# An input projection in 2x2x2 blocks with seven block products, and finished mixes kept in memory

## The chip, the core and the metric

The kernel runs on one core of a Trainium2 chip. The metric is the device time of one execution in microseconds. PE is TensorE (products), DVE is VectorE, ACT is ScalarE, POOL is GpSimd, SP is the engine that issues nearly all DMAs.

## What is computed

One layer of a decoder trunk on 1024 prompt tokens and 8 x 4 sample tokens, d = 1024:

```python
h = rmsnorm(x) * norm_g
b, c, u, z_a, v, z_b = split(h @ w_in)            # w_in: 1024 x 3072, six parts of 512
y_a = b * conv3(c * u) * silu(z_a)                # three taps, with the stored state for the samples
pooled = trailing_mean(v, windows 2/4/8/16) - v   # four groups of 128 channels
y_b = (pooled @ pool_w per group) * pool_scale * silu(z_b)
y = x + concat(y_a, y_b) @ w_out
out = rmsnorm(y) * final_g                        # and the new states of conv and pooling
```

All is float32. A product of two float32 operands is made of three products of the array: each operand is split into a high part of 12 bits and the rest (`split`: ACT copies the high part, DVE subtracts it), and high x low, low x high and high x high are summed.

## The kernel before

Channels lie on the partitions; the 1056 tokens are three thirds of 352 columns (`cols`). `w_in` has 24 column tiles of 128; for each tile and each third `project` issues 24 products (8 contraction chunks x 3 passes) into one PSUM bank, 72 per tile, 1728 in all. The order of the tiles is `M_ORDER`.

- Start: weights of the first three tiles and x arrive in slices by contraction chunk; ACT and DVE apply the gain to x and split it, third by third; PE works on the first three tiles slice by slice (`project_first`). ACT squares x, POOL adds the squares, a product with ones sums them over the channels (`sums_row`), and `rows_rsqrt` makes R, the inverse root mean square of every token, third by third. PE, ACT, DVE and POOL follow the written order in this stretch (`manual_schedule`); behind it a scheduler orders the instructions.
- Loop: tile i + 2 is loaded (512 KB, three buffers `wraw`) and split (three buffers `wt`) while tile i is multiplied. The evacuations multiply each bank by R (`evac`). Behind v come the windows, `pl` and the split `pooled`; behind u the taps `yc`; behind b the finished mix. `pool_linear` multiplies pooled by pool_w. A finished mix is split and stays in the buffers that x and the first weights left.
- Output: w_out is loaded and split per contraction chunk; five token tiles of 128 are done with tokens on the partitions (`po`, the first three together, chunk by chunk), the remaining 416 tokens with channels on the partitions (`pc`); then the residual, the final norm and the stores.

The lines below are those of the profile.

Of the kernel before, what the change touches and what calls it, by code (L numbers as in the profile page):

```python
# [19 lines left out]
NT = 3  # L20
# [33 lines left out]
def trunk(ctx, tc, xt, xres, xct, w_first, w_in, w_out, pool_w, par, fg, sconv, spool,  # L54
# [11 lines left out]
    def tmp(name):  # L66
        return tp.tile([P, TOK], F32, tag="tmp", name=name)
# [4 lines left out]
    # products of ones wake the array while the first operands arrive  # L72
# [6 lines left out]
    # six chunks (of contraction) by 352 tokens in each tile of x  # L79
    xraw = [big.tile([P, 6, TN], F32, tag="mix", name=f"xraw_{i}") for i in range(4)]  # L80

    def x_of(n, k, m=1):
        q = n * KD + k
        return xraw[q // 6][:, q % 6:q % 6 + m, :]

    def load_x(n, k, m):
        nc.sync.dma_start(x_of(n, k, m), xt[:, n * KD + k:n * KD + k + m, :])  # L87

    wfraw = {}

    def load_wf(k, m):
        if k % 2 == 0:
            pool, tag = (wp, "wraw") if k < 6 else (tp, "tmp")
            t = pool.tile([P, 2, WF], F32, tag=tag, name=f"wfraw_{k}")
            wfraw[k], wfraw[k + 1] = t[:, 0, :], t[:, 1, :]
            wfraw[k, 2] = t
        dst = wfraw[k, 2] if m == 2 else wfraw[k].rearrange("p (o c) -> p o c", o=1)
        nc.sync.dma_start(dst, w_first[:, k:k + m, :])  # L98

    for k, m in ((0, 1), (1, 1), (2, 1), (3, 1), (4, 2), (6, 2)):  # L100
        load_wf(k, m)
        load_x(0, k, m)
    load_x(1, 0, 4)
    load_x(1, 4, 4)
# [3 lines left out]
    def load_w(i):  # L108
        t = wp.tile([P, KD, P], F32, tag="wraw", name=f"wraw_{i}")
        nc.sync.dma_start(t, w_in[:, i - NF])  # L110
        wraw[i] = t

    load_x(2, 0, 2)
    load_x(2, 2, 6)
    load_w(NF)
# [8 lines left out]
    nc.vector.tensor_copy(onesr, ones)  # L124

    part = cst.tile([P, C_ALL], F32, name="part")
    nc.sync.dma_start(part, par)
    pwraw = wp.tile([P, NG, P], F32, tag="wraw", name="pwraw")
    nc.sync.dma_start(pwraw, pool_w)
    scb = cst.tile([P, NJ, 6 * NB], F32, name="scb")  # L130
    nc.sync.dma_start(scb[:, :, 0:2 * NB], sconv)
    spb = cst.tile([P, NG, 19 * NB], F32, name="spb")
    nc.sync.dma_start(spb[:, :, 0:15 * NB], spool)
    fgt = cst.tile([P, D], F32, name="fgt")
    nc.sync.dma_start(fgt, fg.partition_broadcast(P))
# [8 lines left out]

# [1 line left out]
    def split(dst, src):  # L146
        """dst[:, 0] = the top 12 bits of src, dst[:, 1] = the rest"""
        nc.scalar.activation(dst[:, 0], src, AF.Copy)  # L148
        nc.vector.tensor_tensor(dst[:, 1], src, dst[:, 0].bitcast(F32), op=ALU.subtract)  # L149

# [1 line left out]
    wfirst = [big.tile([P, 2, 2, NF * P], F32R, tag="mix", name=f"wf_{i}") for i in range(KD // 2)]  # L152
    wt = {}

    def w_of(i, a, k):
        if i < NF:
            return wfirst[k // 2][:, a, k % 2, i * P:(i + 1) * P]
        return wt[i][:, a, k, :]

    def split_w(i):  # L160
        t = wp.tile([P, 2, KD, P], F32R, tag="wt", name=f"wt_{i}")
        split(t, wraw.pop(i))
        wt[i] = t

# [1 line left out]
    xs = [big.tile([P, 2, TOK], F32R, tag="x", name=f"x_{k}") for k in range(KD)]  # L166
    gain = cst.tile([P, KD], F32, name="gain")

    def prep_x(n, k):
        c = cols[n]  # L170
        src = x_of(n, k)[:, 0, :]
        gk = wfraw[k][:, NF * P:] if n == 0 else gain[:, k:k + 1]
        nc.scalar.activation(xs[k][:, 0, c], src, AF.Copy, scale=gk)  # L173
        nc.vector.scalar_tensor_tensor(  # L174
            xs[k][:, 1, c], src, gk, xs[k][:, 0, c].bitcast(F32), op0=ALU.mult, op1=ALU.subtract)

    def prep_first(k):
        w = wfirst[k // 2][:, :, k % 2, :]
        split(w, wfraw[k][:, :NF * P])
        prep_x(0, k)  # L180
        nc.vector.tensor_copy(gain[:, k:k + 1], wfraw[k][:, NF * P:])

    acc = tmp("acc")

    def norm_x(n):
        for k in range(0, KD, 2):
            norm_pair(n, k)

    def norm_pair(n, k):
        c = cols[n]  # L190
        sq = tp.tile([P, 2, TN], F32, tag="tmp", name=f"sq_{n}_{k}")
        nc.scalar.activation(sq, x_of(n, k, 2), AF.Square)  # L192
        if k == 0:
            nc.gpsimd.tensor_tensor(acc[:, c], sq[:, 0], sq[:, 1], op=ALU.add)
        else:
            nc.gpsimd.tensor_tensor(sq[:, 0], sq[:, 0], sq[:, 1], op=ALU.add)
            nc.gpsimd.tensor_tensor(acc[:, c], acc[:, c], sq[:, 0], op=ALU.add)

    def sums_row(sums, name, whole=False):
# [3 lines left out]
        if whole:  # L203
            nc.tensor.matmul(pt, ones, sums, start=True, stop=True)
        else:
            two = tp.tile([P, 2, TC], F32R, tag="tmp", name=f"two_{name}")[:, :, :w]
            split(two, sums)
            for a in (1, 0):
                nc.tensor.matmul(pt, onesr, two[:, a], start=a == 1, stop=a == 0)  # L209
        return pt  # L210

    def rows_rsqrt(out, pt, name):
        """out = (pt / D + eps) ** -0.5, one Newton step behind the table's root;
        the generator lets other work in between the steps"""
# [3 lines left out]
        yield  # L218
        nc.vector.scalar_tensor_tensor(t, pt, D * EPS, out, op0=ALU.add, op1=ALU.mult)  # L219
        yield  # L220
        nc.vector.tensor_tensor(t, t, out, op=ALU.mult)
        yield
        nc.vector.tensor_scalar(t, t, -0.5 / D, 1.5, op0=ALU.mult, op1=ALU.add)
        yield
        nc.vector.tensor_tensor(out, out, t, op=ALU.mult)

# [1 line left out]
    pm = {}  # L228

    def product(i, n, k, a, b, start, stop):  # L230
        nc.tensor.matmul(pm[i, n], w_of(i, a, k), xs[k][:, b, cols[n]], start=start, stop=stop)  # L231

    def project(i, n):
        pm[i, n] = bank(f"pm_{i}_{n}")[:, :TN]
        seq = [(k, a, b) for k in range(KD) for a, b in ((0, 1), (1, 0))]
        seq += [(k, 0, 0) for k in range(KD)]
        for s, (k, a, b) in enumerate(seq):
            product(i, n, k, a, b, s == 0, s == len(seq) - 1)

    def project_first(n, k):  # L240
        if k == 0:
            for i in range(NF):
                pm[i, n] = bank(f"pm_{i}_{n}")[:, :TN]
        for s, (a, b) in enumerate(((0, 0), (1, 0), (0, 1))):
            for i in range(NF):
                product(i, n, k, a, b, k == 0 and s == 0, k == KD - 1 and s == 2)

    def evac1(i, n, out, in1):
        nc.vector.tensor_tensor(out[:, cols[n]], pm[i, n], in1[:, cols[n]], op=ALU.mult)  # L249

    def evac(i, out, in1):
        for n in range(NT):
            evac1(i, n, out, in1)

    mix = []

    def finish_mix(m, name):
        t = big.tile([P, 2, TOK], F32R, tag="mix", name=name)
        split(t, m)
        mix.append(t)  # L260

    def silu(z):
        nc.scalar.activation(z, z, AF.Silu)
        return z

    # group B
    pooled = {}
    szb = {}

    def after_v(g):  # L270
        w = 2 << g
        nc.scalar.copy(spb[:, g, 15 * NB:], vb[:, PM + SEQ:])
# [88 lines left out]
    def scale_rows(n, fill=()):  # L361
        """the rows of chunk n, with the calls of fill in between, then the evacuations"""
        fill = iter(fill)
        for _ in rows_rsqrt(R[:, cols[n]], pr[n], f"{n}"):
            f = next(fill, None)
            if f:
                f()
# [268 lines left out]
```

## Time and profile before

| | before |
|---|---|
| device time, median of 3 runs | 397.25 us (396.31 to 471.15) |
| span of the profiled execution | 394.9 us; its own time isn't listed, the two lower timed runs are 396.31 and 397.25 |
| PE busy | 384.5 us, 97% |
| DVE, ACT, POOL busy | 206.8, 103.8, 24.4 us |
| DMA moved | 31.49 MB |
| granted TensorE clock, mean | 0.990 |

A group of instructions in the profile gives its line, engine, operation, tiles and shape, the count, the busy time and the mean duration of one, and then the idle time just before them with what ended it. PE's products are pipelined: the busy time divided by the count is the pace, the mean duration is longer. The waits say who waited for whom, and the chain goes back from the last instruction through what released each.

### The profile page before, as it was taken

To read this page: it belongs to the slowest core of one execution; us is meant where nothing else is said; L and a number is where in the kernel's file an instruction comes from. 1 tells how busy PE (TensorE), PEld (TensorE's weight loads), DVE (VectorE), ACT (ScalarE), POOL (GpSimd) and SP (SyncE) were. 2 spreads that over 40 slices of the span, in tenths; PEclk is the share of its full clock that TensorE was granted. 3 is DMA by queue.
4 is the path that set the end of the run, shared out by engine and by line. 5 is a ranking of instruction groups with operands and counts; after the bars stand their busy time and mean duration, and the time that the engine had idled before them with its cause. 6 is when DMAs were issued, how large, how long until landed. Compare 5 with 4: busy or idle time off the path is not lost.

```text
span 394.9 us, 5304 instructions
## 1 busy us (share of the span) xinstructions
PE 384.5 (97%) x2238; PEld 370.6 (94%) x2238; DVE 206.8 (52%) x326; ACT 103.8 (26%) x166; POOL 24.4 (6%) x26
## 2 busy tenths in 40 slices
PE   8996999999999999999999999999999999999993
PEld 6996999999999999999999999999998889999883
DVE  4899669994925562326432163322536209322494
ACT  5982407241212230112221022212115106111211
POOL 0394500000000000000000000000000000000000
PEclk9998999999999999999999999999999999999997
DMA  7940131302111101111101111110178301200033
GB/s 245 414 157 1 56 106 55 106 4 78 55 53 56 53 2 53 55 53 55 53 7 48 53 55 53 55 43 15 54 263 296 95 0 54 108 0 0 2 149 130
DMA packets 11783, 31.49 MB, mean 80 GB/s; under 512 B 3568, under 2 KB 4720, under 8 KB 11632
## 3 DMA queue, kind: packets, MB, share of 16 engines
q1 hardware_dynamic: 11616, 30.83, 22.7%
q8 instruction: 17, 0.28, 0.3%
q10 hardware_dynamic: 144, 0.33, 0.2%
q14 instruction: 6, 0.05, 0.0%
HBM read 26.52 MB, written 4.64 MB: 79 GB/s over the span
## 4 chain that ended last, share of the span: by engine, by line
PE 89%; DVE 4%; ACT 2%; DMA 2%; issue 1%; SPq 1%; DVEq 0%
PE pm L231 64%; PE po L466 14%; PE pc L537 9%; DVE x L174 3%; DMA xraw<-in_xt_dram 2%; PE pp L304 1%; ACT x L173 1%; DVE R L217 1%; SPq L98 1%; SPq L87 0%; ACT wf L148 0%; PE pr L209 0%; ACT sq L192 0%; ACT po L475 0%; DVE rt L219 0%
## 5 line engine op out<-in xcount | busy, mean ns | idle before, releaser
L231 PE MATMUL pm<-x,wt 128*128 128x352 f32 x1512 | 244.3, 323 | 0.0
L231 PEld LDWEIGHTS pm<-x,wt 128*128 128x128 f32 x1512 | 243.5, 188 | 0.0
L148 ACT ACTIVATE wt<-wraw 128x1024 fp32r<-128x1024 f32 x21 | 22.2, 1059 | 139.4 <-PE pm L231 120.0
L231 PE MATMUL pm<-x,wf 128*128 128x352 f32 x216 | 38.6, 337 | 3.5 <-DVE x L174 3.1
L231 PEld LDWEIGHTS pm<-x,wf 128*128 128x128 f32 x216 | 36.4, 197 | 5.5 <-DVE x L174 3.9
L149 DVE TENSOR_TENSOR wt<-wraw,wt 128x1024 fp32r<-128x1024 f32 x21 | 25.7, 1223 | 10.1 <-ACT wt L148 10.1
L466 PE MATMUL po<-wo,mixa 128*128 128x512 f32 (+1 forms) x132 | 28.8, 374 | 0.0
L466 PE MATMUL po<-wo,mixb 128*128 128x512 f32 (+1 forms) x132 | 28.8, 373 | 0.0
L466 PEld LDWEIGHTS po<-wo,mixa 128*128 128x128 f32 x132 | 23.4, 189 | 4.5
L466 PEld LDWEIGHTS po<-wo,mixb 128*128 128x128 f32 x132 | 23.4, 189 | 4.4
L249 DVE TENSOR_TENSOR vb<-pm,t 128x352 f32<-128x352 f32 x12 | 6.3, 524 | 32.2 <-PE pm L231 32.2
L488 POOL TENSOR_TENSOR zg<-zt,fgt 128x256 f32<-128x256 f32 x1 | 0.7, 722 | 344.6 <-DVE zt L474 344.6
L249 DVE TENSOR_TENSOR t<-pm,R 128x352 f32<-128x352 f32 x12 | 6.3, 525 | 29.3 <-PE pm L231 29.3
L537 PE MATMUL pc<-mixb,wo 128*128 128x416 f32 x96 | 19.4, 351 | 0.0
L537 PE MATMUL pc<-mixa,wo 128*128 128x416 f32 x96 | 19.4, 350 | 0.0
L249 DVE TENSOR_TENSOR ya<-pm,sza 128x352 f32<-128x352 f32 x12 | 6.3, 524 | 25.0 <-PE pm L231 25.0
L474 DVE TENSOR_TENSOR zt<-po,zt 128x512 f32<-128x512 f32 (+1 forms) x11 | 7.0, 641 | 21.7 <-PE po L466 21.6
L537 PEld LDWEIGHTS pc<-mixb,wo 128*128 128x128 f32 x96 | 17.9, 188 | 0.3
L537 PEld LDWEIGHTS pc<-mixa,wo 128*128 128x128 f32 x96 | 18.0, 188 | 0.2
L174 DVE SCALAR_TENSOR_TENSOR x<-xraw,gain,x 128x352 fp32r<-128x352 f32 x16 | 17.3, 1136 | 0.4 <-ACT x L173 0.4
L148 ACT ACTIVATE wo<-woraw 128x1024 fp32r<-128x1024 f32 x8 | 8.3, 1057 | 32.7 <-PE pm L231 28.0
L475 ACT ACTIVATE po<-zt 128x512 f32<-128x512 f32 (+1 forms) x11 | 6.1, 557 | 33.6 <-DVE zt L474 33.6
(102 smaller groups left out, 271.4 us busy)
## 6 DMA issues: line engine op xcount, KB each, us to landing
wraw<-in_w_in_dram SPq DMA_DIRECT2D x21, 512.0 KB, 3.3
woraw<-in_w_out_dram SPq DMA_DIRECT2D x8, 512.0 KB, 3.6
zt<-in_xres_dram SPq DMA_DIRECT2D x5, 512.0 KB, 7.2
out_yt_dram<-zt SPq DMA_DIRECT2D x4, 512.0 KB, 2.6
xraw<-in_xt_dram SPq DMA_DIRECT2D x2, 704.0 KB, 8.1
xraw<-in_xt_dram SPq DMA_DIRECT2D x3, 352.0 KB, 6.7
xraw<-in_xt_dram SPq DMA_DIRECT2D x1, 1056.0 KB, 10.7
zc<-in_xct_dram SPq DMA_DIRECT2D x1, 832.0 KB, 4.4
```

What stands on the lines that cost most here:

```text
L98: nc.sync.dma_start(dst, w_first[:, k:k + m, :])
L148: nc.scalar.activation(dst[:, 0], src, AF.Copy)
L149: nc.vector.tensor_tensor(dst[:, 1], src, dst[:, 0].bitcast(F32), op=ALU.subtract)
L173: nc.scalar.activation(xs[k][:, 0, c], src, AF.Copy, scale=gk)
L174: nc.vector.scalar_tensor_tensor(xs[k][:, 1, c], src, gk, xs[k][:, 0, c].bitcast(F32), op0=ALU.mult, op1=ALU.subtract)
L217: nc.vector.reciprocal(out, t)
L231: nc.tensor.matmul(pm[i, n], w_of(i, a, k), xs[k][:, b, cols[n]], start=start, stop=stop)
L249: nc.vector.tensor_tensor(out[:, cols[n]], pm[i, n], in1[:, cols[n]], op=ALU.mult)
L466: nc.tensor.matmul(pt, mix[k][:, b, t * P:(t + 1) * P], wo[k][:, a, c], start=(k == 0 and s == 0), stop=(k == KD - 1 and s == 2))
L474: nc.vector.tensor_tensor(z[:, c], pt, z[:, c], op=ALU.add)
L475: nc.scalar.activation(pt, z[:, c], AF.Square, accum_out=ss[:, i:i + 1])
L537: nc.tensor.matmul(pt, wo[k][:, a, d * P:(d + 1) * P], mix[k][:, b, T0:], start=(k == 0 and s == 0), stop=(k == KD - 1 and s == 2))
```

## The change

The first two column tiles (v 0 and zb 0, `NF = 2`) are done as before, but with the gain applied to the weights. The other 22 tiles form 11 pairs (`PAIRS`): (c, u), (za, b), (v, zb). For a pair the thirds 0 and 1 of the tokens are the two block rows of A (A11, A12, A21, A22: token third x half of the contraction), the two tiles and the two halves of the contraction are the blocks B11, B12, B21, B22, and the product is made from seven block products of 12 products each:

| bank | accumulates | left and right tile of thirds 0 and 1 |
|---|---|---|
| a | B11 A11, later + B21 A12 | left of third 0 = a; s1 is a copy of a's first part |
| b | T2 S2, later + T3 S3, + T4 A22 | t1 = b + s1, t2 = b + s1 one block later; left of third 1 = b + s1 at the end |
| c | T1 S1, later + B22 S4 | right of third 1 = c + t2; right of third 0 = c + t1 at the end |

Third 2 (`pl`) is done with the plain blocks, 48 products (`l`, `r`). S1 to S4 are sums and differences of the A blocks, made and split once at the start (1408 columns each); T1 to T4 (`tw`) are those of the pair's B blocks. Each pair's weights are loaded into the only buffer `wraw` (1 MB), multiplied by the gain on ACT, and split into four units wa, wb, wc, wd that go round five buffers `wt`. POOL, which added squares before, now makes some of the multiplications by R (`gt`). R comes from squares in another layout (token tiles, `xres` loaded a second time) by way of a diagonal matrix and three products with ones. Seven of the eight finished mixes go to memory (`spill`) and are loaded and split again ahead of the output projection.

The diff, cut to its core:

```diff
-NF = 3
-M_ORDER = [("v", 0), ("zb", 0), ("zb", 1), ("v", 1), ("v", 2), ("zb", 2), ("v", 3), ("zb", 3)]
-M_ORDER += [(q, j) for j in range(NJ) for q in ("c", "u", "za", "b")]
-E_ORDER = [4, 5, 6, 7, 0, 1, 2, 3]
+PAIRS = [(("v", 0), ("zb", 0)), (("c", 0), ("u", 0)), (("za", 0), ("b", 0)),
+         (("v", 3), ("zb", 3)), (("c", 1), ("u", 1)), (("za", 1), ("b", 1)),
+         (("v", 2), ("zb", 2)), (("c", 2), ("u", 2)), (("za", 2), ("b", 2)),
+         (("v", 1), ("zb", 1)), (("c", 3), ("u", 3)), (("za", 3), ("b", 3))]
+NF = 2
+E_ORDER = [4, 0, 7, 1, 6, 2, 5, 3]
...
+    def load_w(p):
+        t = wp.tile([P, 4, KH * P], F32, tag="wraw", name=f"wraw_{p}")   # wp: one buffer
+    def gain_w(p):                                     # 8 x ACT, 256 columns, in place
+    def make_t(p):
+        nc.vector.tensor_tensor(t[:, 0:2], w[:, 2:4], w[:, 0::2], op=ALU.subtract)
+        nc.vector.tensor_tensor(t[:, 2], w[:, 3], t[:, 0], op=ALU.subtract)
+        nc.vector.tensor_tensor(t[:, 3], w[:, 1], t[:, 2], op=ALU.subtract)
+    def make_unit(p, u):
+        t = wp.tile([P, 2, 2, KH * P], F32R, tag="wt", bufs=5, name=f"w{u}_{p}")
...
+    def strassen(p, S1, S2, S3, S4, hooks):
+        block(a, p, "B11", A11, True, False)
+        nc.scalar.copy(s1, a)
+        block(b, p, "T2", S2, True, False)
+        vt(t1, b, s1, op=ADD)
+        block(c, p, "T1", S1, True, False)
+        vt(left[:, n2], pL, scale[:, n2], op=MUL)      # behind plain l
+        hooks["early"]()          # load_w, gain_w, make_t, unit a of pair p + 1
+        block(a, p, "B21", A12, False, True)
+        vt(left[:, n0], a, scale[:, n0], op=MUL)
+        block(b, p, "T3", S3, False, False)
+        vt(t2, b, s1, op=ADD)
+        vt(right[:, n1], c, t2, op=ADD)                # then plain r
+        hooks["middle"]()         # units d and c of pair p + 1
+        block(b, p, "T4", A22, False, True)
+        vt(left[:, n1], b, s1, op=ADD)
+        gt(left[:, n1], left[:, n1], scale[:, n1], op=MUL)
+        block(c, p, "B22", S4, False, True)
+        vt(right[:, n0], c, t1, op=ADD)
+        hooks["late"]()           # unit b of pair p + 1
...
+        make_unit(1, "a")                              # the written order of the start
+        make_unit(1, "b")
+        squares_last(acc)
+        vt(S1f, raw[1][:, :KH], raw[1][:, KH:], op=ADD)
+        vt(S3f, raw[0][:, :KH], raw[1][:, :KH], op=ALU.subtract)
+        split(S1, S1f)
+        split(S3, S3f)
+        for t in range(NTT):
+            square2(t, sq[t])
+        vt(S2f, S1f, raw[0][:, :KH], op=ALU.subtract)
+        split(S2, S2f)
+        make_t(1)
+        make_unit(1, "d")
+        block(pL, 1, "B11", pl[0], True, False)        # and B21, then pR with B12, B22
+        sums_rest(acc)
+        diag = rows()
+        rows_out(diag)
+        make_unit(1, "c")
...
+            nc.sync.dma_start(d, m)                    # finish_mix: seven of eight mixes
...
+    for k in range(KD):                                # ahead of the output projection
+        nc.sync.dma_start(wr, w_out[:, k])
+        split(wo[k], wr)
+        nc.sync.dma_start(mr, spill[k])
+        split(mix[k], mr)
```

Three places where the order of the instructions matters follow. A row gives the line, the operation, the tile written and those read, the shape, and the engines waited for.

PE before, between the first tiles: third 2 of tiles 1 and 2 (`pm_2_442`, `pm_2_501`), and between them the row sums of third 1 (`pr_467`):

```order
L231 MATMUL pm_2_442<-x_144,wf_137 128x352
L231 MATMUL pm_2_442<-x_145,wf_137 128x352
L209 MATMUL pr_467<-two_468,onesr 128x352 [waits DVE_49]
L209 MATMUL pr_467<-two_468,onesr 128x352 [waits Activation_49]
L231 MATMUL pm_2_501<-x_138,wf_134 128x352 x2
L231 MATMUL pm_2_501<-x_139,wf_134 128x352 x2
```

PE of the change, behind the first tiles: plain products of pair 1 (`l_423`, `r_448`), the sums of squares (`rest`), the row products (`pr`), then pair 1's blocks (`a_534`, `b_581`):

```order
L228 MATMUL l_423<-pl_139,wa_374 128x352 x12
L228 MATMUL r_448<-pl_138,wb_377 128x352 [waits PE_49,Activation_49]
L228 MATMUL r_448<-pl_138,wb_377 128x352 [waits DVE_49]
L228 MATMUL r_448<-pl_138,wb_377 128x352 x10
L228 MATMUL r_448<-pl_139,wb_377 128x352 x12
L266 MATMUL rest<-ones,acc 128x1 [waits DVE_49]
L266 MATMUL rest<-ones,acc 128x1 [waits Activation_49] x2
L266 MATMUL rest<-ones,acc 32x1 [waits Activation_49]
L292 MATMUL pr_503<-diag,ones 128x352 [waits DVE_49]
L292 MATMUL pr_506<-diag,ones 128x352 [waits DVE_49,Activation_49]
L292 MATMUL pr_509<-diag,ones 128x352 [waits DVE_49,Activation_49]
L228 MATMUL a_534<-A_134,wa_374 128x352 [waits Activation_49]
```

What moved: the rows of all tokens now stand in one piece behind the plain products, and pair 1's first block stands behind them in PE's queue; before, each third's sums stood between products that didn't need them.

DVE of the change at the same place, ahead of that diagonal: the last sums for S2 and S4 (`raw_89`, `S4f`), S2's low part (`S_413`), the T blocks (`tw_416`), unit d, then the rows:

```order
L507 TENSOR_TENSOR raw_89<-raw_88,raw_89 128x1408
L510 TENSOR_TENSOR S4f_409<-raw_89 128x704 [waits DVE_49]
L510 TENSOR_TENSOR S4f_410<-raw_89 128x704 [waits Activation_49]
L154 TENSOR_TENSOR S_413<-raw_89,S_413 128x1408 [waits Activation_49]
L207 TENSOR_TENSOR tw_416<-wraw_229 128x1024
L208 TENSOR_TENSOR tw_416<-wraw_229,tw_416 128x512 [waits DVE_49]
L209 TENSOR_TENSOR tw_416<-wraw_229,tw_416 128x512 [waits DVE_49]
L154 TENSOR_TENSOR wd_420<-tw_416,wd_420 128x1024 [waits Activation_49]
L274 TENSOR_SCALAR ms<-ss 128x9 [waits Activation_49]
L276 RECIPROCAL r_483<-u_484 128x9 [waits Activation_49]
```

DVE before, in the rows of third 1: evacuations of the banks, a weight split, and the root's inverse:

```order
L249 TENSOR_TENSOR vb<-pm_1_299,R 128x352 [waits DVE_49,PE_49]
L249 TENSOR_TENSOR szb_148<-pm_1_300,R 128x352 [waits PE_49]
L249 TENSOR_TENSOR szb_149<-pm_1_301,R 128x352 [waits PE_49]
L149 TENSOR_TENSOR two_577<-acc,two_577 128x352 [waits Activation_49]
L149 TENSOR_TENSOR wt_584<-wraw_582,wt_584 128x1024 [waits DMAHW6_49,Activation_49]
L149 TENSOR_TENSOR pws<-pwraw,pws 128x512 [waits DMAHW2_49,Activation_49]
L217 RECIPROCAL R<-rt_589 128x352 [waits Activation_49]
```

What moved: the rows' arithmetic came between evacuations and one weight split; now it stands behind all of S1 to S3, the T blocks and unit d.

DVE of the change in pair 4 (c 1, u 1), behind the windows of v 3: `pl_1084` and `pooled`, left of third 2 (`t_1096`), the T blocks and unit a of pair 5 (`tw_1177`, `wa_1181`), left of third 0, then t2 (`t_4_1209`):

```order
L352 SCALAR_TENSOR_TENSOR pl_1084<-win_1_1073,vb 128x1024 [waits DVE_49]
L358 TENSOR_TENSOR first_1087<-win_1_1073,part 128x15
L359 TENSOR_TENSOR pl_1084<-first_1087,vb 128x15 [waits DVE_49]
L154 TENSOR_TENSOR pooled_1_1091<-pl_1084,pooled_0_1090 128x1056 [waits Activation_49]
L433 TENSOR_TENSOR t_1096<-l_1141,R_132 128x352 [waits PE_49]
L207 TENSOR_TENSOR tw_1177<-wraw_1167 128x1024 [waits DMAHW7_49,Activation_49]
L154 TENSOR_TENSOR wa_1181<-wraw_1167,wa_1181 128x1024 [waits Activation_49]
L208 TENSOR_TENSOR tw_1177<-wraw_1167,tw_1177 128x512 [waits DVE_49]
L437 TENSOR_TENSOR t_1096<-a_1098,R_132 128x352 [waits PE_49]
L209 TENSOR_TENSOR tw_1177<-wraw_1167,tw_1177 128x512 [waits DVE_49]
L440 TENSOR_TENSOR t_4_1209<-b_1113,s_4_1111 128x352 [waits PE_49]
```

DVE before in the loop, at a c and a u tile (`t_1556`, `vb`) with the splits between:

```order
L149 TENSOR_TENSOR mixa_1473<-ya_1469,mixa_1473 128x1056 [waits Activation_49]
L249 TENSOR_TENSOR t_1556<-pm_0_1476,R_133 128x352 [waits PE_49]
L249 TENSOR_TENSOR t_1556<-pm_1_1501,R_133 128x352 [waits PE_49]
L249 TENSOR_TENSOR t_1556<-pm_2_1526,R_133 128x352 [waits PE_49]
L149 TENSOR_TENSOR wt_1637<-wraw_1635,wt_1637 128x1024 [waits DMAHW3_49,Activation_49]
L249 TENSOR_TENSOR vb<-pm_0_1560,t_1556 128x352 [waits DVE_49,PE_49]
```

What moved: before, a bank is read once, behind its last product, and a split of the tile after next stands between; now t2 reads bank b between two blocks that accumulate in it, behind the T blocks and unit a of the next pair.

More of the change, by code (lines that the diff above doesn't have):

```diff
@@ L153, in trunk @@
[L153 to L185, printed above, removed]
-        for k in range(0, KD, 2):
[L187 to L197, printed above, removed]
@@ L201, in sums_row, with rows_out @@
+    def rows_out(diag):
+        for n in range(NT):
+            pt = bank(f"pr_{n}")[:, :TN]
+            nc.tensor.matmul(pt, ones, diag[:, cols[n]], start=True, stop=True)
+            nc.scalar.copy(R[:, cols[n]], pt)
+        nc.scalar.activation(R2, R, AF.Square)
+    def sums_row(sums, name):
         w = sums.shape[1]
         pt = bank(f"pr_{name}")[:, :w]
[L203 to L209, printed above, removed]
+        two = [tp.tile([P, TOK], F32R, tag="tmp", name=f"two_{a}_{name}")[:, :w] for a in range(2)]
+        split2(two[0], two[1], sums)
+        for a in (1, 0):
+            nc.tensor.matmul(pt, onesr, two[a], start=a == 1, stop=a == 0)
@@ new lines, in trunk @@
+            split_x(2, k, 1)
+            project_first(2, k)
+        nc.vector.tensor_copy(gain.rearrange("p (k o) -> p k o", o=1), wfraw[:, :, 2 * P:])
+        load_w(1)
+        nc.sync.dma_start(part, par)
+        sq = [square(t) for t in range(NTT)]
+        for n in (0, 1):
+            for k in range(0, KD, 2):
+                split_x(n, k, 2)
+            for k in range(KD):
+                project_first(n, k)
+        for i in range(2):
+            nc.scalar.copy(heads[i][:, n2], pm[i, 2])
@@ new lines, in trunk, with early, middle, late @@
+        for i in range(2):
+            gt(heads[i][:, n2], heads[i][:, n2], R[:, n2], op=MUL)
+    nc.sync.dma_start(scb[:, :, 0:2 * NB], sconv)
+    nc.sync.dma_start(spb[:, :, 0:15 * NB], spool)
+    pwraw = tmp("pwraw")[:, :NG * P].rearrange("p (g c) -> p g c", c=P)
+    nc.sync.dma_start(pwraw, pool_w)
+    linear = {}
+    for p in range(1, NP):
+        nxt = p + 1 < NP
+        def early():
+            if nxt:
+                load_w(p + 1)
+                gain_w(p + 1)
+                make_t(p + 1)
+                make_unit(p + 1, "a")
+        def middle():
+            if nxt:
+                make_unit(p + 1, "d")
+                make_unit(p + 1, "c")
+        def late():
+            if nxt:
+                make_unit(p + 1, "b")
+        hooks = {"early": early, "middle": middle, "late": late}
+        if p == 1:
+            def first():
+                split(pws, pwraw)
+                after_v(0)
+                silu(szb[0])
+            hooks["plain"] = (pL, pR)
+            hooks["first"] = first
+        strassen(p, S1, S2, S3, S4, hooks)
+        if PAIRS[p - 1][0][0] == "v":
+            pool_linear(PAIRS[p - 1][0][1])
@@ L554, in chan_tail @@
             nc.sync.dma_start(yc_out[:, d0:d0 + m, :], zc[d0, m])
+    for t in range(len(first), NTT):
+        load_zt(t)
     for t in range(len(first), NTT):
```

483 lines of the change are left out of this document (272 added, 211 removed).

## Prediction

> **What bounds the kernel now.** I read the page's busy line, then the chain that ended last in order of time.
>
> ```profile
> PE 384.5 (97%) x2238; PEld 370.6 (94%) x2238; DVE 206.8 (52%) x326; ACT 103.8 (26%) x166; POOL 24.4 (6%) x26
> 35.65 7.25 PE pm L231 x34
> ...
> 134.30 162.22 PE pm L231 x1008
> 296.52 33.30 PE po L466 x144
> ...
> 388.82 0.02 issue
> ```
>
> From 35.65 us to 388.82 us the chain hardly leaves TensorE (PE). 1008 products of 352 columns take 162.22 us, 0.161 us each, so the 1728 of the input projection cost 278.2 us. The output projection, 296.52 to 388.82, is 92.3 us, the tail to the span's end 6.1 us, and the 36 pooling products 5.8 us. That makes 382.4 of 394.9; the other 12.5 us are PE's waits in the first 36 us. So PE work removed counts in full, as long as the vector engine (DVE), the scalar engine (ACT) and GpSimd (POOL) stay ahead. How much room have they?
>
> ```profile
> 0.00:10.00 10.00, 8.99 (x38) 6.12 (x39) 4.68 (x15) 5.70 (x10) 0.20 (x4) 1.00 0.78 246
> 10.00:20.00 10.00, 9.83 (x62) 9.54 (x61) 8.90 (x19) 9.50 (x19) 4.11 (x4) 1.00 1.03 413
> 150.00:200.00 50.00, 50.00 (x313) 50.00 (x312) 17.73 (x25) 7.66 (x10) 0.00 (x0) 1.00 0.15 49
> L149 DVE TENSOR_TENSOR wt<-wraw,wt 128x1024 fp32r<-128x1024 f32 x21 | 25.7, 1223 | 10.1 <-ACT wt L148 10.1
> L149 DVE TENSOR_TENSOR pws<-pwraw,pws 128x512 fp32r<-128x512 f32 x1 | 0.7, 687 | 0.0
> L249 DVE TENSOR_TENSOR t<-pm,R 128x352 f32<-128x352 f32 x12 | 6.3, 525 | 29.3 <-PE pm L231 29.3
> L282 DVE TENSOR_TENSOR win<-vb 128x1038 f32<-128x1038 f32 x4 | 4.9, 1234 | 0.0
> L148 ACT ACTIVATE wt<-wraw 128x1024 fp32r<-128x1024 f32 x21 | 22.2, 1059 | 139.4 <-PE pm L231 120.0 <-issue 19.4
> L192 ACT ACTIVATE sq<-xraw 128x704 f32<-128x704 f32 x12 | 9.3, 780 | 5.3 <-DVE R L225 3.7 <-POOL acc L197 1.6
> L475 ACT ACTIVATE po<-zt 128x256 f32<-128x256 f32 x2 | 0.8, 388 | 4.2 <-DVE zt L474 4.2
> L216 ACT ACTIVATE rt<-pr,eps 128x352 f32<-128x352 f32 x3 | 1.6, 547 | 9.9 <-PE pr L209 9.9
> L148 ACT ACTIVATE pws<-pwraw 128x512 fp32r<-128x512 f32 x1 | 0.6, 617 | 0.0
> L409 ACT ACTIVATE R<-R 128x1056 f32<-128x1056 f32 x1 | 1.1, 1087 | 4.6 <-DVE R L225 4.6
> L475 ACT ACTIVATION_READ_ACCUMULATOR po<-zt 128x1 f32 x11 | 2.1, 187 | 0.0
> ```
>
> Columns of the stretches: length, then PE, PEld, DVE, ACT and POOL busy, clock, DMA share, GB/s. In the middle DVE is 35% busy. At 10 to 20 us DVE and ACT are 89% and 95% busy: the start has no room.
>
> **What goes.** A pair of column tiles cost 2x3x24 = 144 products; now it is seven block products of 12 and four plain ones of 12, 132. Over 11 pairs 132 products go: 132 x 0.161 = 21.3 us. The plain fp32 row products of the start (three, 0.75 us each by the row below) replace shorter ones; I charge them in the start.
>
> ```profile
> L204 PE MATMUL pr<-acc,ones 128*128 128x352 f32 x2 | 0.8, 458 | 0.0
> ```
>
> **The start.** PE's queue now holds the plain products of pair 1 (l, r), then the four sums, then three row products, and only behind these pair 1's blocks. So everything waits for the diagonal that the row products read, and DVE makes it behind the S matrices.
>
> ```profile
> 14.73 0.58 DVE L174 SCALAR_TENSOR_TENSOR x<-xraw,wfraw,x 128x352 fp32r<-128x352 f32 x1
> ```
>
> PE: that was the last low part of the first token third, 15.3 us. Now a slice is 312 KB where 377 KB came, and its weights are 256 columns for 384; I put the end of its 48 products at 14 us (12.5 by the bytes alone, 16 if nothing gets shorter). 96 more and the 48 of l and r: 14 + 144 x 0.161 = 37.2 us.
>
> DVE and ACT: 5.38 MB (eight slices, two thirds of x) must land before the last split; with 2.46 MB in the first 10 us and 413 GB/s after, 17.1 us. From there, one behind the other:
> - ACT: two splits of 704 (0.78), two copies of 352 (0.55), a square of 512 (0.6), eight gains of 256 (0.388 each, 0.33 back to back): 23.1.
> - wa and wb: ACT 1.06, then DVE twice 1.22 (on an engine that waits for nothing about 0.08 of it overlaps the next): 26.6.
> - The four squares of the last third share one buffer, since eight tmp tiles are taken: 0.5 + 3 x (0.78 + 2 x 0.525) and hops: 32.7.
> - 1408 columns are not in the trace. From 352 to 1024 columns DVE gains 1.04 ns a column and ACT about 0.72, so 1.6 and 1.34 us. Bounds: 1.22 and 1.06 (1024), and twice 704, 1.8 and 1.56. S1 and S3, two sums and two splits on DVE, S3's high part on ACT at 37.3. ACT then squares five tiles (1.06 + 0.187, 1.2 together) before S2's high part: 44.7; DVE's low part 46.3.
> - tw (1.22 + 2 x 0.69) 48.9; wd ACT and DVE 51.2; four sums handed from PE to ACT one by one, 52.0; root, Newton step, first three diagonal blocks 54.1.
> - Row products and their copies: pair 1 begins at 56.4.
>
> PE is ready at 37.2, so it waits **17 us**, then is 2 us on rows. From below the cost is bounded by DVE's own work: from 20 us, where the last split of x ends, it has 24 us to do (2.3 for wa and wb, 4.1 of squares, 9.4 on 1408 columns, 1.6 for S4, 2.5 tw, 1.2 wd, 3 for the rows), which puts the diagonal at 44, 10 us earlier. From above, a 1408-column operation at twice 704 adds 2 us.
>
> **Pair 1.** 84 + 9 products are 15.0 us. ACT has R2 (1.08), S4 and wc before the third block may start, 61.1. DVE does wc, five evacuations of 0.525, a window of 1.23 and pl of 1.22 before t1 at 68.2, while PE could begin T3S3 at 65.4; then tw, wa and pooled stand before the pooling products (71.7 for 70.2). I count 5.6 us of waits (0 if ACT and DVE were ahead, 9 if nothing overlaps) and pair 1 ends at 77.0.
>
> **Pairs 2 to 11.** 1320 products and 27 for pooling: 212.5 + 4.4 us. A pair lasts 21.2 us. DVE has eight evacuations of 0.45 back to back, 2.4 us of tw and four unit splits of 1.14, 10.6 us; with 7.9 for v 3 (four windows, pl, pooled), 4.2 for c (two taps, three pooling evacuations) and 2.4 for z, three pairs make 46 us of 65. POOL adds ten multiplications of 352-column size.
>
> ```profile
> L174 DVE SCALAR_TENSOR_TENSOR x<-xraw,gain,x 128x352 fp32r<-128x352 f32 x16 | 17.3, 1136 | 0.4 <-ACT x L173 0.4
> L174 DVE SCALAR_TENSOR_TENSOR x<-xraw,wfraw,x 128x352 fp32r<-128x352 f32 x8 | 4.7, 584 | 1.1 <-ACT x L173 1.1
> 17.22 14.06 DVE L174 SCALAR_TENSOR_TENSOR x<-xraw,gain,x 128x352 fp32r<-128x352 f32 x12 [0.22 <-ACT x L173]
> L196 POOL TENSOR_TENSOR sq<-sq 128x352 f32<-128x352 f32 x9 | 11.0, 1223 | 4.3 <-ACT sq L192 4.3
> 37.87 0.94 POOL L196 TENSOR_TENSOR sq<-sq 128x352 f32<-128x352 f32 x1 [3.59 <-ACT sq L192]
> L488 POOL TENSOR_TENSOR zg<-zt,fgt 128x256 f32<-128x256 f32 x1 | 0.7, 722 | 344.6 <-DVE zt L474 344.6
> ```
>
> The same DVE operation takes 0.584 us without POOL and 1.17 (14.06/12) beside it; POOL's goes from 0.94 to 1.22. From 256 and 352 columns POOL's 704 is about 1.75 and its 1056 about 2.55 us, and I let DVE operations on two SBUF inputs wait for these. The Trainium skill, SBUF — State Buffer, "Who interferes with whom", says that such an operation and a GpSimd one that reads SBUF exclude each other for the whole instruction. By that rule the pitch would be 0.58 + 0.94 = 1.5 us; the trace shows 1.17, so the block is partial and the measurement decides. Without any block the waits of the pairs below would be about half, 3.5 us less.
>
> What sets the pair's waits is one chain: the single wraw buffer is free when wb is split, then the next 1 MB loads, ACT applies eight gains, DVE makes tw and wa, and behind these stands t2, without which T4A22 cannot start 17.3 us into the pair.
>
> ```profile
> wraw<-in_w_in_dram SPq DMA_DIRECT2D x21, 512.0 KB, 3.3
> xraw<-in_xt_dram SPq DMA_DIRECT2D x2, 704.0 KB, 8.1
> zc<-in_xct_dram SPq DMA_DIRECT2D x1, 832.0 KB, 4.4
> ```
>
> From 512 and 832 KB I take 5.1 us for 1 MB (3.3 at least, 8.1 at most). After z: wb at 2.0, load 7.2, gains 9.9, tw 11.1, two evacuations, tw's rest and wa, t2 at 15.3: 2 us to spare. After c: wb waits for POOL (3.2), POOL's yc holds tw to 12.0, t2 at 18.7 against 18.8 (the pooling products give 1.45 us): nothing to spare. After v 3, DVE has right's last evacuation at 4.3 and wb at 5.45, gives way to POOL's 704 to 7.2, then does two windows (9.6), t1, the last window and pl (12.45). ACT's high part of pooled (1.08) waits for that, and six of the eight gains stand behind it: gains at 15.9, tw 17.1, wa 18.2, t2 at 20.3, a wait of 3.0 us. After v 2, one window less but all eight gains behind pooled, 2.4; after v 1, 1.0. With 0.7 in pair 2 that is **7.1 us** (0 if DVE is quicker, about 23 at 8.1 us).
>
> **The turn to the output projection** reloads seven spilled tiles and splits them beside wo: 2.3 us of DVE per chunk against 4.16 of PE (33.30/8). Only mix 0's low part is late, about 1 us (0 to 4). The 7.6 MB of spills lie on queues used at 49 GB/s; on SP each store stands behind the next load, so no load waits for it. Hidden, as long as loads come a pair early.
>
> **Sum.** 56.4 + 15.0 + 5.6 + 212.5 + 4.4 + 7.1 + 1.0 + 92.3 + 6.1 = 400.4 us of span, against 394.9. The undisturbed timed runs, 396.31 and the median 397.25, lie 1.4 and 2.35 above the profiled span; with 1.9 the forecast is **402 us**, 1.2% slower: 21.3 us of PE work go and 25 come back as waits.
>
> **Rivals.**
> 1. *Slower: the load chain decides every pair.* If 1 MB takes 8.1 us, pairs 2, 5 and 8 lose 3 each, 3, 6 and 9 0.9 each, 4, 7 and 10 5 together: 16 us, 418 us. Against it, the 832 KB row; for it, spills and units now share the queues, and the after-c pairs have no slack. From about 6 us of landing the kernel is over 2% slower.
> 2. *Faster: the start runs at DVE's own sum and the pairs keep up.* Less 9.9, 5.6, 7.1 and 1: 379 us. For it, 46 us of DVE work in 65. Against it, ACT and DVE hand each S matrix to one another in turn, and both engines take work strictly in order.
>
> PE's clock after the gap is no rival of its own:
>
> ```profile
> PE pm L231 <- DVE x L174: 3.1, 2, 2.8
> ```
>
> ```profile
> 36.00:37.00 1.00, 1.00 (x5) 1.00 (x5) 0.90 (x3) 0.00 (x0) 0.00 (x0) 0.50 0.00 0
> ```
>
> The first row is of the waits (total, times, longest): PE stood 2.8 us for x, just ahead of 35 us. Behind that it was granted 0.50 for some 3 us, 1.5 us of work. Behind the new gap that falls on pair 1's first two blocks, whose successor waits for wc anyway; uncovered it costs 1.5 us. That the product count doesn't fall is excluded by the code.
>
> **How the numbers follow.** Forecast 0.56 (own range 394 to 408, of it 0.04 above the 2% line), rival 1 0.32, rival 2 0.12. Two per cent, 389.3 to 405.2, is about what a measurement of this kernel can tell from no change. Faster 0.12, same 0.52, slower 0.36. The range 391 to 415 leaves out rival 2 and the end of rival 1.
>
> **What would show it.** A gap of PE near 37 to 54 us, ended by DVE's diagonal (right), or by another thing (wrong); a low granted clock just behind it; PE waits on t2 in the pairs behind v; 1 MB landing in about 5 us; about 1 us before po. A gap under 10 us, or pairs of 21.2 us throughout, would make me wrong on the fast side, pairs of 23 us on the slow side.

## Result and the profile after

The changed kernel takes **399.96 us** (median of 4, 399.89 to 400.16), the kernel before 397.19 us on the same chip: ratio 1.0089, 95% interval 1.0068 to 1.0110. One of the four runs of the kernel before took 471.15 us, and the ratio leaves it out. The difference is real and small: 0.9% slower. The profiled execution took 399.92 us, 2.0 us more than its span of 397.9 us.

The busy line, two lines of the 40 slices and the loads of the weights (count, size, median us to landing), from the page of the changed kernel:

```profile
PE 371.4 (93%) x2114; PEld 353.8 (89%) x2114; DVE 268.7 (68%) x404; ACT 174.1 (44%) x297; POOL 42.0 (11%) x31
...
PE   9998058899999999999999999999999999999993
...
PEclk9999559899999999999999999999999999999999
...
wraw<-in_w_in_dram SPq DMA_DIRECT2D x11, 1024.0 KB, 4.7
```

PE was busy for 384.5 us of 394.9 and is now busy for 371.4 of 397.9. So 13.1 us of busy time went, and idle time rose by 16.1, from 10.4 to 26.5 us: +3.0 us of span. The slices show where: the fifth and sixth, 40 to 60 us, are 0 and 5 tenths busy, at half clock. The waits of PE (total, times, longest), and its timeline there (start, length; in brackets the idle time before and what ended it):

```profile
PE rest L266 <- ACT ss L267: 13.3, 3, 12.8
PE b L228 <- DVE t L426: 2.6, 1, 2.6
PE pr L292 <- DVE diag L285: 2.5, 1, 2.5
...
PE po L613 <- DVE mix L154: 0.2, 1, 0.2
```

```profile
38.42 0.28 PE L266 MATMUL rest<-ones,acc 128*128 128x1 f32 x2
51.46 0.59 PE L266 MATMUL rest<-ones,acc 128*128 128x1 f32 x2 [12.76 <-ACT ss L267]
...
55.94 3.89 PE L292 MATMUL pr<-diag,ones 128*128 128x352 f32 x6 [2.54 <-DVE diag L285]
59.19 3.33 PE L228 MATMUL a<-A,wa 128*128 128x352 f32 x12
```

PE has done pair 1's plain products at 38.4 us and begins its blocks at 59.2. The wait stands at the sums (`rest`), whose little copies (`ss`) come on ACT behind the squares of five tiles and the high parts of S1 to S3 and wd; then comes the diagonal. From 80 us on all is different:

```profile
80.00:298.00 218.00, 217.89 (x1348) 217.60 (x1348) 154.53 (x208) 91.98 (x153) 37.07 (x22) 1.00 0.21 78
```

In this stretch of pairs 2 to 11 (length; PE, PEld, DVE, ACT, POOL; clock, DMA share, GB/s) PE is busy for 217.89 us of 218.00, at full clock.

### The profile page after: what moved, and what is told of

Same layout as the page of the kernel before. It is cut to its first block, busy times and chain, and to the rows that moved or that the text cites. A ratio compares the mean times of both kernels' runs of the same rounds, so it can differ in the third digit from the quotient of the medians.

```text
span 397.9 us, 5295 instructions
## 1 busy us (share of the span) xinstructions
PE 371.4 (93%) x2114; PEld 353.8 (89%) x2114; DVE 268.7 (68%) x404; ACT 174.1 (44%) x297; POOL 42.0 (11%) x31
## 4 chain that ended last, share of the span: by engine, by line
PE 74%; DVE 11%; ACT 7%; DMA 4%; issue 2%; SPq 1%; POOL 1%; DVEq 0%; ACTq 0%; POOLq 0%
PE b L228 14%; PE po L613 13%; PE pc L685 9%; PE r L228 9%; PE c L228 9%; PE a L228 9%; PE l L228 9%; DMA raw<-in_xt_dram 4%; PE pp L369 2%; DVE win L347 2%; ACT wraw L202 2%; ACT xk L239 1%; PE pr L292 1%; DVE tw L207 1%; DVE wa L154 1%
## 5 line engine op out<-in xcount | busy, mean ns | idle before, releaser
L613 PE MATMUL po<-wo,mix 128*128 128x512 f32 (+1 forms) x264 | 56.7, 375 | 0.2 <-DVE mix L154 0.2
L613 PEld LDWEIGHTS po<-wo,mix 128*128 128x128 f32 x264 | 46.2, 188 | 10.2 <-DVE mix L154 0.9
L228 PE MATMUL a<-A,wa 128*128 128x352 f32 x264 | 47.5, 329 | 0.0
L228 PEld LDWEIGHTS a<-A,wa 128*128 128x128 f32 x264 | 44.2, 192 | 0.6 <-ACT R L293 0.4
L228 PE MATMUL l<-pl,wa 128*128 128x352 f32 x264 | 44.5, 324 | 0.0
L228 PE MATMUL r<-pl,wb 128*128 128x352 f32 x264 | 44.5, 324 | 0.0
L202 ACT ACTIVATE wraw<-wraw,gain 128x256 f32<-128x256 f32 x88 | 36.7, 497 | 17.4 <-DMA wraw<-in_w_in_dram 16.4
L228 PEld LDWEIGHTS l<-pl,wa 128*128 128x128 f32 x264 | 43.0, 188 | 0.0
L228 PEld LDWEIGHTS r<-pl,wb 128*128 128x128 f32 x264 | 43.0, 188 | 0.0
L685 PE MATMUL pc<-mix,wo 128*128 128x416 f32 x192 | 36.5, 352 | 0.0
L228 PE MATMUL b<-S,wd 128*128 128x352 f32 x132 | 23.1, 324 | 0.0
L228 PE MATMUL c<-S,wb 128*128 128x352 f32 x132 | 23.1, 324 | 0.0
```

What stands on the lines that cost most here:

```text
L202: nc.scalar.activation(t, t, AF.Copy, scale=gain[:, k:k + 1])
L228: nc.tensor.matmul(pt, t[:, a, i, k * P:(k + 1) * P], x[:, b, k], start=first and s == 0, stop=last and s == len(seq) - 1, skip_group_chec ...
L613: nc.tensor.matmul(pt, mix[k][:, b, t * P:(t + 1) * P], wo[k][:, a, c], start=(k == 0 and s == 0), stop=(k == KD - 1 and s == 2))
L685: nc.tensor.matmul(pt, wo[k][:, a, d * P:(d + 1) * P], mix[k][:, b, T0:], start=(k == 0 and s == 0), stop=(k == KD - 1 and s == 2))
```

## Experiments

**Theory A**: the start took the gain. Everything that S and T need for pair 1 is made by DVE and ACT in turn, while PE has nothing to do; the pairs keep what they save. **Rivals**: only the place of the rows in the queue is at fault (B); POOL and DVE hold each other up in the pairs; the load chain; spills and the single buffer cost time that doesn't show as a wait. The edits are shown shortened: a `+` line is what this run has, a `-` line what it has no longer.

**1. Rows first.** The squares, the rows and their products stand ahead of S1 to S4, tw and wd.

```
+ five squares, l and r, sums_rest(acc); diag = rows(); rows_out(diag)
  S1f, S3f, S2f, S1, S3, S2, tw, wd, S4, wc
- five squares; l and r, sums_rest(acc); diag = rows(); rows_out(diag)
```

> The squares, the rows and their three products stand ahead of S1 to S4, tw and wd on every engine; nothing else changes. Theory A (the gap of PE ahead of pair 1, 38.4 to 59.2 us, is the whole chain of DVE and ACT work for S, tw, wd and the rows; the rows are only its last piece): the rows' products come near 46 us, but T2 S2 then waits for S2 and wd, which come as late as before or a little later, near 64 us. No gain: 399 to 403 us. Rival B (the order in PE's queue alone costs the gap, since the rows hold back blocks whose operands are ready): some 15 us less, 384 us.

Measured: 400.17 us, ratio to before 1.0107 (1.0071 to 1.0143), as the changed kernel itself. PE's timeline:

```profile
43.04 3.42 PE L292 MATMUL pr<-diag,ones 128*128 128x352 f32 x6 [2.55 <-DVE diag L285]
45.83 2.86 PE L228 MATMUL a<-A,wa 128*128 128x352 f32 x12
50.99 2.20 PE L228 MATMUL a<-A,wa 128*128 128x352 f32 x12 [2.30 <-ACT s L418]
61.94 0.66 PE L228 MATMUL b<-S,wd 128*128 128x352 f32 x1 [8.75 <-ACT wd L153]
```

The rows come 12.9 us earlier, and the time stays: the wait has moved to T2 S2, which needs wd, and that begins at 61.9 us. B falls. Whichever of the two is first, the other is late: the S and T work of both engines must be done before pair 1 can run.

**2. POOL's multiplications in the pairs to DVE.**

```
- gt(left[:, n1], ...); gt(right[:, both], ...); gt(up[:, 2:2 + 2 * TN], ...); yc on gpsimd
+ vt(left[:, n1], ...); vt(right[:, both], ...); vt(up[:, 2:2 + 2 * TN], ...); yc on vector
```

> The multiplications of the pairs that POOL makes go to DVE. Theory A (pairs 2 to 11 run at PE's pace in the trace: 1347 products in 218 us, so neither POOL nor DVE sets their time): within 1 us, 399 to 401 us. The prediction's chain with a block between POOL and DVE: also no gain, since its waits did not come. Rival C (DVE at 68% is close to its limit, POOL relieves it): 6 to 10 us more, since DVE gets ten operations of 0.44 us per three pairs and after v it is late: 406 to 410 us.

Measured: 398.92 us, ratio 1.0095 (1.0063 to 1.0126); the span is 0.8 us shorter. The ratio doesn't differ from the changed kernel's 1.0089 by more than the intervals, so rival C falls, and POOL doesn't set the pairs.

**3. Each load of 1 MB from pair 3's on twice.**

```
- nc.sync.dma_start(t, w_in[...])
+ for _ in range(2 if p > 2 else 1): nc.sync.dma_start(t, w_in[...])
```

> From pair 3's weights on, each 1 MB load is made twice, one behind the other, so that it lands some 4 to 5 us later. The prediction's rival 1 (the load, the gains, tw and t2 are one chain that T4 A22 waits for, over 2% slower from a landing of about 6 us on): with the slack that the trace shows for t2 (1.6 us in pair 2, 2.8 in pair 3, none in pair 4) the pairs lose 2 to 4 us each, 15 to 25 us in all: 415 to 425 us. Theory D (there is room, since units come free early): under 405 us.

Measured: 418.47 us, ratio 1.0581 (1.0521 to 1.0641). Its busy line, its waits and its loads:

```profile
PE 378.1 (91%) x2114; PEld 356.5 (86%) x2114; DVE 273.7 (66%) x404; ACT 171.3 (41%) x297; POOL 40.2 (10%) x31
...
PE rest L267 <- ACT ss L268: 13.3, 3, 12.8
PE b L229 <- DVE wd L155: 7.7, 6, 1.5
```

```profile
wraw<-in_w_in_dram SPq DMA_DIRECT2D x20, 1024.0 KB, 4.9
```

Nine loads are made twice, so that each lands some 4.9 us later, and the span grows by 18.1 us to 416.0, 2.0 each. Of these, 11.4 us are idle time of PE; the other 6.7 are the same 2114 products taking longer (378.1 us busy for 371.4), at a lower clock behind the waits: the mean granted clock from 85 to 300 us is 0.98, where the changed kernel had 1.00 from 80 to 298. The slower rival's mechanism is real. It has some 2.9 us of slack on average (4.9 less 2.0), where my chain had none behind c and v; not all of that is slack of the changed kernel, since the waits are now at T2 S2 and no longer at T4.

**4. Pair 1 with plain blocks, in the gap.** Pair 1 (c 0 and u 0) makes all three thirds with 144 plain products, which need wa and wb alone; the squares of both kinds alternate on ACT, v 0 and z_b 0 leave their banks as copies by ACT and are multiplied by R later, the rows stand between the plain blocks, and the S and T blocks are made for pair 2 meanwhile. Ten pairs keep the seven products.

```
+ plain1(1); squares; sums_rest(acc); S1, S3; plain1(2); rows; rows_out; plain1(0)
+ S2, S4f; make_t(2), units a, d, S4, unit c of pair 2
- make_t(1), units d, c of pair 1
- for p in range(1, NP): strassen(p, ...)
+ for p in range(2, NP): strassen(p, ...)
```

It ran twice: the first run meets chunks 0 and 4 of `w_out` with each other's mix, the second takes them in the order in which the mixes now finish.

> Pair 1 is done with plain blocks on all tokens (144 products where it had 132), in the stretch in which PE stood; its T blocks are left out, the squares and rows come between, and pair 2's units and S are made meanwhile. Theory A (the cost of the change is the start's gap, 20.8 us, and pair 1's waits, 5.7 us): pair 2 begins near 57 to 60 us instead of 80.1, less 12 products more: 378 to 383 us. Rival E (the gap is DVE's work and only moves on: evacuations and windows of the first tiles come on top of pair 2): 390 us or more.

> Pair 1 again with plain blocks in TensorE's gap (10 pairs by seven block products, no T blocks for pair 1), the two first output chunks taken in the order in which their mixes finish. Theory A (the gap of the start is where the gain went, and the pairs keep theirs): 382 to 384 us, as the run of this kind before. Rival (the pairs lose part of it again, and the time before was helped by something else): above 388.

Measured: 382.93 us, ratio 0.9680 (0.9656 to 0.9704), and 382.88 us, ratio 0.9665 (0.9646 to 0.9684). The second one's busy line, clock and PE's longest waits:

```profile
PE 367.1 (96%) x2126; PEld 351.1 (92%) x2126; DVE 265.9 (70%) x394; ACT 172.1 (45%) x298; POOL 41.4 (11%) x28
...
PEclk9999999999999999999999999999999999999999
```

```profile
PE b L228 <- ACT wd L153: 2.8, 1, 2.8
...
PE b L228 <- DVE t L429: 1.7, 1, 1.7
```

12 products *more* than the changed kernel, and 17 us less (16 to 17 by the ratios, since the runs are of different chips). Its PE is even less busy (367.1 for 371.4 us), since nothing runs at half clock: without these 12 products it would be 365.2, so that some 6.2 us of the changed kernel's busy time are the price of the low clock (an estimate from the two busy lines).

**5. All pairs plain.** No S, no T, and POOL's multiplications in the pairs go to DVE; the single buffer, the gains and the spills stay.

```
- b: T2 S2 | T3 S3 | T4 A22;  c: T1 S1 | B22 S4;  make_t, units c and d
+ for n in (2, 0, 1): l, r: block(B11/B12, blocks[n, 0]), block(B21/B22, blocks[n, 1])
```

> All pairs with plain blocks, 144 products each; no S matrices, no T blocks. The single buffer for the 1 MB loads, the gains on the scalar engine and the spills stay. Theory A (spills, loads and gains are hidden, and each pair by seven block products saves its full 12 products): 383 + 120 x 0.161 less about 5 us of waits that the S and T blocks made in the start = 397, range 395 to 399, that of the kernel before. Rival 1 (spills and the single buffer cost time in every pair): 401 or more. Rival 2 (the block products lose part of their saving to waits in the pairs): 390 to 394.

Measured: 396.30 us, ratio 0.9997 (0.9984 to 1.0011).

```profile
PE 386.3 (98%) x2246; PEld 371.9 (94%) x2246; DVE 188.0 (48%) x306; ACT 145.6 (37%) x271; POOL 14.9 (4%) x12
```

This is the time of the kernel before, so what was added beside the scheme costs nothing on balance (single costs and gains may hide each other in it). Against it, experiment 4 has 120 products less: PE is busy for 19.2 us less (120 x 0.161 is 19.3), stands idle for 5.4 us more (13.5 for 8.1), and the span falls by 13.8, from 394.4 to 380.6. The pairs by seven products keep their saving.

**6. Half of pair 2's gains earlier** (from the second kernel of 4).

```
+ gain_w(2, range(4)); split S1; sums_rest(acc); split S3; gain_w(2, range(4, KD))
- sums_rest(acc); split S1; split S3; ...; gain_w(2)
```

> As the kernel with a plain pair 1, but half of pair 2's gains stand ahead of S1's split on the scalar engine, the other half behind S3's, in time in which it waited for the sums. The scalar engine is then some 3 us earlier at R and at wa, the vector engine's S4 sums come ahead of GpSimd's multiplication that stretched them from 1.69 to 4.00 us, and pair 2's blocks find wd ready. Theory A (the waits left in the start, 2.8 + 0.6 us at wd and 1.6 at T3 S3, are the hand-overs between the two engines): 377.5 to 380.5 us. Rival (another operation of the vector engine is late at the same place): 382 to 384.

Measured: 383.53 us, ratio 0.9680 (0.9664 to 0.9696). That is the rival's range, not theory A's. ACT came no earlier in the profiled run, since pair 1's load landed 2 us later in it (the gains began at 23.7 us, where the second kernel of 4 had 21.5):

```profile
23.68 3.31 ACT L202 ACTIVATE wraw<-wraw,gain 128x256 f32<-128x256 f32 x8 [1.56 <-DMA wraw<-in_w_in_dram]
```

The S4 sums didn't come ahead of POOL either, for DVE first waited for R and then multiplied v by it:

```profile
49.83 1.26 DVE L554 TENSOR_TENSOR vb<-vb,R 128x1056 f32<-128x1056 f32 x1 [0.59 <-ACT R L296]
51.01 4.01 DVE L535 TENSOR_TENSOR S4f<-raw 128x704 f32<-128x704 f32 x2
```

PE's wait for wd grew from 2.8 to 3.7 us, and the 11 products behind it took 2.75 us, where they took 1.94 in the second kernel of 4:

```profile
60.90 0.43 PE L228 MATMUL b<-S,wd 128*128 128x352 f32 x1 [3.68 <-ACT wd L153]
61.17 2.75 PE L228 MATMUL a<-A,wa 128*128 128x352 f32 x11
```

**7. The first z_b times R on DVE** (from the second kernel of 4 again), behind wb's split.

```
- gt(szb[0], szb[0], R, op=MUL)
+ vt(szb[0], szb[0], R, op=MUL)      # behind make_unit(2, "b")
```

> As the kernel with a plain pair 1, but the first z_b's multiplication by R (1056 columns) goes from GpSimd to the vector engine, which does it behind wb's split. Theory A (GpSimd's operation and the vector engine's two S4 sums shut each other out, so that the sums take 4.00 us for 1.69): the sums take about 1.7 us again, wd is ready 2.3 us earlier and PE's wait for it falls from 2.8 to about 0.5 us; behind wb the vector engine has 1.25 us more, so that t1 comes 1 us earlier only, and of the 2.3 us about 1 is left: 381 to 382.5 us. Rival (the sums are long for another reason, such as their own operands): they stay at 4.0 us, and the time is 383 to 384.

Measured: **381.94 us**, ratio 0.9630 (0.9613 to 0.9646), the fastest here. DVE's two sums and POOL's multiplication in the second kernel of 4, then DVE's and PE's timelines of this run:

```profile
48.74 4.00 DVE L534 TENSOR_TENSOR S4f<-raw 128x704 f32<-128x704 f32 x2
...
49.37 2.63 POOL L554 TENSOR_TENSOR szb<-szb,R 128x1056 f32<-128x1056 f32 x1 [48.06 <-ACT R L296]
```

```profile
49.15 1.70 DVE L534 TENSOR_TENSOR S4f<-raw 128x704 f32<-128x704 f32 x2
```

```profile
58.09 0.43 PE L228 MATMUL b<-S,wd 128*128 128x352 f32 x1 [0.97 <-ACT wd L153]
...
75.07 2.21 PE L228 MATMUL b<-S,wc 128*128 128x352 f32 x12 [1.66 <-DVE t L429]
...
80.25 2.04 PE L228 MATMUL a<-A,wa 128*128 128x352 f32 x11 [0.83 <-DVE wa L154]
```

The sums take 1.70 us where they took 4.00 beside POOL, and the wait for wd falls from 2.8 to 1.0 us. 0.9 us of time is left of it: DVE has the 1.25 us of z_b to do ahead of t1, so that T3 S3 waits for t1 as before (1.66 us), and in the next pair PE waits 0.83 us for wa.

## Why the prediction was right, and where it was not

The forecast was 402 us, the kernel took 399.96. The sign is right, and so is the mechanism of the start; the waits of the pairs are not. That the sum comes so near is partly luck: the start was 2.8 us too short and the pairs 5.9 us too long. The prediction took two per cent for about what a measurement can tell; the interval here is 0.2% to either side.

| step | predicted | measured |
|---|---|---|
| PE ready for pair 1's blocks | 37.2 | 38.4 |
| pair 1 begins | 56.4 | 59.2 |
| pair 1, products and waits | 20.6 | 20.95 |
| pairs 2 to 11, with pooling | 224.0 | 218.1 |
| the turn and the output projection | 93.3 | 93.4 |
| tail | 6.1 | 6.3 |
| span | 400.4 | 397.9 |

- **The start, 2.8 us too early.** The gap is where it was put; 12.8 us of it end with the copies of the sums and the last 2.5 with the diagonal, in the order in which the prediction has them. ACT's timeline shows where the first 1.9 us come from:

```profile
19.11 1.47 ACT L153 ACTIVATE A<-raw 128x704 fp32r<-128x704 f32 x2 [0.25 <-DMA raw<-in_xt_dram]
...
21.71 3.31 ACT L202 ACTIVATE wraw<-wraw,gain 128x256 f32<-128x256 f32 x8
```

  The last slice of x is split from 19.1 us, where I had it landed at 17.1, and eight gains take 3.3 us (0.41 each, I had 0.33 and so 2.6): they end at 25.0 for 23.1. The first diagonal blocks are then ready at 55.9 for 54.1. The rest is the clock. I let its low stretch fall on pair 1's blocks, but the row products meet it first: 3.25 us to pair 1's begin, where I had 2.3. PE's stretches of the changed kernel:

```profile
56.00:59.00 3.00, 3.00 (x5) 1.73 (x6) 1.00 (x6) 0.77 (x2) 0.00 (x0) 0.50 0.00 0
59.00:61.00 2.00, 2.00 (x7) 1.67 (x6) 0.69 (x1) 1.81 (x5) 0.61 (x1) 0.50 0.03 8
```

- **Pair 1: 20.95 us for 20.6, by other terms.** T3 S3 waits for t1, 2.6 us as against 2.8. But the pooling products wait 0.15 us where I had 1.5, and PE doesn't wait for wc. In their place stands the clock, which I had put at nothing here, since the wait for wc would hide it:

```profile
70.94 3.35 PE L228 MATMUL b<-S,wc 128*128 128x352 f32 x12 [2.55 <-DVE t L426]
...
91.77 2.11 PE L228 MATMUL b<-S,wc 128*128 128x352 f32 x12
```

  The 12 products of T3 S3 take 3.35 us behind the wait, in pair 2 without a wait 2.11; the mean granted clock from 65 to 80 us is 0.89. With pair 1's first block, still at 0.50 until 61 us, and the pooling products the low clock costs about 3.0 us of pair 1 (an estimate: 20.95 less 93 products of 0.1617 and 2.9 us of waits). That the two sums agree is luck.
- **The pairs, the term that failed: 7.1 us of waits, measured 0.1 in the stretch shown above.** (The products took 0.1617 us each where I had 0.161, which takes 1 us back.) The step is the one for the pair behind v 3, "DVE has right's last evacuation at 4.3 and wb at 5.45". Pair 4 begins at 122.81:

```profile
117.64 1.22 DVE L154 TENSOR_TENSOR wc<-tw,wc 128x1024 fp32r<-128x1024 f32 x1
...
123.81 0.52 DVE L455 TENSOR_TENSOR szb<-c,t 128x352 f32<-128x352 f32 x1
124.25 1.22 DVE L154 TENSOR_TENSOR wb<-wraw,wb 128x1024 fp32r<-128x1024 f32 x1
125.38 2.74 DVE L347 TENSOR_TENSOR win<-win 128x1036 f32<-128x1036 f32 x1
...
132.54 1.08 ACT L153 ACTIVATE pooled<-pl 128x1056 fp32r<-128x1056 f32 x1 [1.32 <-DVE pl L359]
133.53 2.50 ACT L202 ACTIVATE wraw<-wraw,gain 128x256 f32<-128x256 f32 x6
...
139.97 0.52 DVE L440 TENSOR_TENSOR t<-b,s 128x352 f32<-128x352 f32 x1
```

  Counted from the pair's begin, right's last evacuation ends at +1.5 us and wb at +2.7, 2.8 us earlier than predicted. From there the chain runs as predicted, pooled's high part and six gains ahead of tw: it comes 2.6 us earlier, t2 at +17.7 for my +20.3, and T4 A22 begins at 140.55 with hardly a wait. The load isn't on this chain, since ACT stood 1.32 us for pl after two gains. The prediction doesn't write out what it put ahead of that evacuation. A split of wc would be one such thing: it ends 4 us ahead of the pair's begin, still in the pair before. But it is 1.2 us of the 2.8; where the rest came from stays open. That the pairs behind v 2 and v 1 had no wait either is shown by the stretch; their chains weren't followed step by step.
- **The turn.** PE waits 0.2 us for mix 0, where I had 1.0. That the turn still takes 93.4 us for 93.3 comes from slightly slower products (the first 144 take 33.8 us, 33.3 before).
- **By its own signs** the prediction has the gap and the low clock behind it right, and 1 MB landing in about 5 us. The waits on t2 behind v and the 1 us before po did not come, and pairs of 21.3 us throughout (101.47 to 122.81, for one) are what it named as the sign of being wrong on the fast side.
- **The slower rival** (0.32) has a mechanism that is real (experiment 3), but 1 MB lands in 4.7 us and not in 6 or more. **The faster rival** had pairs that keep up, which is what they do; but its start at DVE's own sum, 44 us, was far off, and in experiment 1 too, with the rows out of the way, T2 S2 waits until 61.9 us.
- **"21.3 us of PE work go and 25 come back"** holds in kind, not in its parts: nearly all comes back in the first 80 us. The 132 products are worth 21.3 us, yet only 13.1 us of busy time went, mainly because some 6.2 us of low clock came in (the estimate in experiment 4). Experiment 4 shows that it needn't be so: given other work in that time, PE keeps 13 to 14 us.

## What to carry to other kernels

A scheme that saves products on the bound engine must have its operands made by others, and here the first use paid for that with nearly all of the saving. Look first for what the bound engine can do without them: here one stage done the plain way, 12 products dearer, with the start ordered around it, was worth 16 to 17 us. Where a wait is counted, count the products behind it too: in experiment 3 a third of the loss was products at a lower clock. And a sum that comes out right should be taken apart stage by stage: the waits in the pairs, 7.1 us, never came, because DVE stood 2.8 us earlier than the evaluation had it.

## What the runs showed of the hardware

- Behind the gap (12.8 us and then 2.5 us of idle time) PE's granted clock was 0.50 from 56 to 61 us. The six records of the row products sum to 3.9 us there, and to 1.9 us in experiment 4, which has no gap ahead of them. A low clock puts its price on whatever stands first behind the gap. How long a wait it takes is not settled here: the 2.6 us at T3 S3 were followed by slow products, the 2.8 us for wd in the second kernel of 4 were not (1.00 from 59 to 61 us), and the 3.7 us in experiment 6 were.
- DVE and POOL, each on two SBUF operands, shut each other out almost fully here, where I had read a partial block from the trace of before. Pair 4's wb and window stand beside the first of these two; the second is undisturbed:

```profile
124.41 2.62 POOL L460 TENSOR_TENSOR szb<-szb,R 128x704 f32<-128x704 f32 x1 [1.79 <-DVE szb L455]
...
146.81 1.71 POOL L463 TENSOR_TENSOR up<-um,t 128x704 f32<-128x704 f32 x1
```

  POOL's 704 columns begin beside wb's split, which runs to 125.47, and end at 127.03; DVE's window of 1.24 us, from 125.38, ends at 128.12, 1.1 us behind POOL. The three durations stand one behind the other, but for some 0.15 us at each hand-over: POOL ends 1.56 us behind wb, where it takes 1.71 undisturbed, and the window 1.09 behind POOL. Two such hand-overs for each pair of operations would make 1.22 us of the 0.58 and 0.94 us of before, which ran at 1.17; so the two traces need not differ (an estimate, which no run here isolates). This exclusion is what the Trainium skill, SBUF — State Buffer, "Who interferes with whom", says of such a pair, and experiment 7 gives its price: 2.3 us on two sums. In the pairs it cost nothing that PE shows, idle for 0.11 of 218 us, and moving POOL's work to DVE changed nothing either (experiment 2).
